# Bias rows of the attention: stored to DRAM once, then copied from DRAM to DRAM, one head at a time

## Chip, cores and metric

The kernel runs on one core of a Trainium2 chip. The metric is the time of one execution on the device in microseconds (us); lower is better. Engines are named as the profile names them: PE (TensorE, matmuls), DVE (VectorE), ACT (ScalarE), POOL (GpSimd) and SP (SyncE, which here only issues DMAs). POOL's DMAs go through the queue software_dynamic (q0), SP's through hardware_dynamic (q1); both are carried by the same 16 DMA engines.

## The reference

Two layers, each of three parts that add to x (512 tokens of width 1024, float32):

```python
for l in range(DEPTH):          # DEPTH = 2
    x = x + 0.5 * swiglu_ffn(rms_norm(x, ffn1_norm_w[l]), ffn1_w_gate[l], ffn1_w_up[l], ffn1_w_down[l])
    x = x + hybrid_mixer(rms_norm(x, mix_norm_w[l]), l, ...)
    x = x + 0.5 * swiglu_ffn(rms_norm(x, ffn2_norm_w[l]), ffn2_w_gate[l], ffn2_w_up[l], ffn2_w_down[l])
```

The mixer runs an mLSTM, a state-space branch with convolutions, and a differential attention of four heads, and projects their outputs back. What the change touches is the bias of the attention, which depends only on the distance of query and key:

```python
rel = q_pos[:, None] - k_pos[None, :]
bias = rel_bias[t5_bucket(rel)]            # per head
logits = (q @ k.T) * scale + bias          # -inf where rel < 0
```

## The kernel before

**Phases.** The list PHASES runs f1, mx, f2 for layer 0 and again for layer 1: `ffn`, `mixer`, `ffn`. Activations stay in SBUF with the 1024 features on 8 tiles of 128 partitions x 512 tokens.

**Matmuls.** Every large product is made of three matmuls (`mm3`, L127 to L129) of operands that are split into a high and a low part. Weights come in blocks of 1 MB: `load` (L108) lets SP fetch a block into `raw`, of which there are two buffers; `split` (L121, L122) casts half a block on ACT into `whi` and subtracts on DVE into `wlo`, of each of which there are three buffers. So SP can issue a block only when the block two before it has been split, and a split waits until PE is done with the one three before it. In the first FFN, PE needs about 11 us for a block: the loop over f runs 22 blocks for gate and up, and 11 more follow for the down product.

**The bias.** `build_bias(h)` is called inside the first FFN of layer 0, at f = 3, 5, 7 and 9, for h = 0 to 3. For h = 0 it multiplies a one-hot matrix `oh` with `rel_bias` in two small matmuls, which gives one row of 640 values per head, and copies them to `bias_row`, a tile of 4 partitions in SBUF. Each call then lets POOL copy one head's row 128 times into `bias_dram[h]` (128 x 640 values, 320 KB). The mixer reads it back with a step of 639 in `load_pair` (L510), so that each of 128 partitions of the tile `T` gets its row shifted by one; T is added to the logits in `soft` (L528), ACT makes the exponentials `pt` (L531) from them, PE transposes these (L545), ACT copies them to `aT` (L547) and PE multiplies with the values (L556).

**Order.** The order of the instructions on each engine is not written by hand. A scheduler places the whole program, both layers in one piece, by its own estimates of durations and of when tiles come free; `load`, `split` and the first loads ask it for a high priority. Each engine, and each DMA queue's issuing engine, then works its list from top to bottom and waits at semaphores. The mixer of layer 0 and that of layer 1 are the same code, but their orders differ in the kernel before. Apart from the weights SP and POOL issue in a mixer: the stores of q and k to `qk_dram` (L402) and their reload as `st` (L504), T (L510), the mask loads `sS` (L631) with the row added to them (L632), and the like for `D` (L748, L749).

Of the kernel before, what the change touches and what calls it, by code (L numbers as in the profile page):

```python
# [10 lines left out]
F32 = mybir.dt.float32  # L11
# [3 lines left out]
ALU = mybir.AluOpType  # L15
# [4 lines left out]
P = 128  # L20
# [8 lines left out]
NEG = -1.0e30  # L29
NREL = 640  # L30
# [14 lines left out]
def hybrid_kernel(ctx, tc, aps, phases):  # L45
    nc = tc.nc
    pe, act, dve, pool = nc.tensor, nc.scalar, nc.vector, nc.gpsimd

    const = ctx.enter_context(tc.tile_pool(name="const", bufs=1))
# [7 lines left out]
    dram = ctx.enter_context(tc.tile_pool(name="dram", bufs=1, space=DRAM))  # L57

    def acc():
        return acc_pool.tile([P, S], F32, name="acc", tag="acc")  # L60

    def aux():
        return aux_pool.tile([P, S], F32, name="aux", tag="aux")
# [40 lines left out]
    def load(src, soon=True):  # L104
        n = src.shape[1]
        with tc.high_priority() if soon else nullcontext():
            raw = wp.tile([P, 2 * WPC], F32, name="raw", tag="raw", bufs=2)
            nc.sync.dma_start(out=raw[:, :n], in_=src)  # L108
        return raw

    def split(raw, lo, n, eng=dve):
        return split_parts(raw, ((lo, n),), eng)

    def split_parts(raw, parts, eng=dve):
        with tc.high_priority():
            hi = wp.tile([P, WPC], F32R, name="whi", tag="whi", bufs=3)
            lw = wp.tile([P, WPC], F32R, name="wlo", tag="wlo", bufs=3)
            to = 0
            for lo, n in parts:
                t = slice(to, to + n)  # L120
                act.copy(hi[:, t], raw[:, lo:lo + n])  # L121
                eng.tensor_tensor(lw[:, t], raw[:, lo:lo + n], hi[:, t].bitcast(F32), ALU.subtract)  # L122
                to += n
        return hi, lw

    def mm3(out, lh, ll, rh, rl, first, last):
        pe.matmul(out, lh, rh, start=first, stop=False)  # L127
        pe.matmul(out, lh, rl, start=False, stop=False)  # L128
        pe.matmul(out, ll, rh, start=False, stop=last)  # L129


    def prep(d, wcol):
        w = pv[:, wcol + d:wcol + d + 1]
        act.activation(xh[d], x[d], AF.Copy, scale=w)
        dve.scalar_tensor_tensor(xl[d], x[d], w, xh[d].bitcast(F32), ALU.mult, ALU.subtract)  # L135
        if d == 0:
            act.activation(sqacc, x[d], AF.Square)
        else:
            sq = tp.tile([P, S], F32, name="sq", tag="t0", bufs=2)
            act.activation(sq, x[d], AF.Square)  # L140
            dve.tensor_tensor(sqacc, sqacc, sq, ALU.add)
# [16 lines left out]
    def rms_of_x():  # L158
        ps = aux()
        for j in range(NB):  # L160
            pe.matmul(ps[:, j:j + 1], sqacc[:, j * P:(j + 1) * P], ones[:, 0:1], start=True, stop=True)
        rst = tp.tile([P, NB], F32, name="rst", tag="rst", bufs=2)
        dve.tensor_copy(rst, ps[:, 0:NB])
        rstd(rst, DM)
        return rst

    def spread(rst):
        pb = aux()
        for j in range(NB):
            pe.matmul(pb[:, j * P:(j + 1) * P], rst[:, j:j + 1].broadcast_to([P, P]), ident, start=True, stop=True)  # L170
        act.copy(rsb, pb)


    def ffn(l, which, nxt, first):
        with tc.tile_pool(name=f"g{l}{which}", bufs=1) as gp:
            gh, gl = [], []
            for f in range(KF):
                if f == 0:

                    halves = [((512 * r, 512), (1024 + 512 * r, 512)) for r in range(2)]  # L180
                    raw = raw0 if first else load(aps["wgu"][l, which, f])
                    pp = [acc(), aux()]
                    for r in range(2):
                        hi, lw = split_parts(raw, halves[r])
                        for k in range(4):
                            if 4 * r + k == KD - 1:
                                rst = rms_of_x()
                            for u in range(2):
                                c = slice((u * 4 + k) * P, (u * 4 + k + 1) * P)
                                mm3(pp[u], hi[:, c], lw[:, c], xh[4 * r + k], xl[4 * r + k], 4 * r + k == 0, 4 * r + k == KD - 1)  # L190
                    spread(rst)
                else:
                    raw = load(aps["wgu"][l, which, f], f > 1 or not first)
                    pp = []
                    for u in range(2):
                        hi, lw = split(raw, u * 1024, 1024)
                        ps = aux() if u else acc()
                        for k in range(KD):
                            c = slice(k * P, (k + 1) * P)
                            mm3(ps, hi[:, c], lw[:, c], xh[k], xl[k], k == 0, k == KD - 1)  # L200
                        pp.append(ps)
                if first and 3 <= f <= 9 and f % 2:
                    build_bias(f // 2 - 1)
                gs = tp.tile([P, S], F32, name="gs", tag="t0", bufs=2)
                dve.tensor_tensor(gs, pp[0], rsb, ALU.mult)  # L205
                act.activation(gs, gs, AF.Silu)
                us = tp.tile([P, S], F32, name="us", tag="t1", bufs=2)
                dve.tensor_tensor(us, pp[1], rsb, ALU.mult)  # L208
                dve.tensor_tensor(us, us, gs, ALU.mult)
                h = gp.tile([P, S], F32R, name=f"gh{f}")  # L210
                lo = gp.tile([P, S], F32R, name=f"gl{f}")
                act.copy(h, us)
                dve.tensor_tensor(lo, us, h.bitcast(F32), ALU.subtract)
                gh.append(h)
                gl.append(lo)
            ps = None
            for c in range(KD * KF // 16):
                raw = load(aps["wdn"][l, which, c])
                for half in range(2):
                    hi, lw = split(raw, half * 1024, 1024)  # L220
                    for s in range(8):
                        d, k = divmod(c * 16 + half * 8 + s, KF)
                        if k == 0:
                            ps = aux() if d % 2 else acc()
                        cc = slice(s * P, (s + 1) * P)
                        mm3(ps, hi[:, cc], lw[:, cc], gh[k], gl[k], k == 0, k == KF - 1)
                        if k == KF - 1:
                            dve.scalar_tensor_tensor(x[d], ps, 0.5, x[d], ALU.mult, ALU.add)
                            if nxt is None:
                                nc.sync.dma_start(out=aps["out"][:, d, :], in_=x[d])  # L230
                            else:
                                prep(d, nxt)


    bias_dram = dram.tile([4, P, NREL], F32, name="bias_dram")
# [1 line left out]
    row_dram = dram.tile([DEPTH, 12, S], F32, name="row_dram")  # L237
    qk_dram = dram.tile([2, 2, 2, 4, 32, S], F32, name="qk_dram")

    bias_row = const.tile([4, NREL], F32, name="bias_row")  # L240

    def build_bias(h):

        if h == 0:
            with tc.tile_pool(name="bb", bufs=1) as bp:
                oh = bp.tile([33, NREL], F32, name="oh")
                nc.sync.dma_start(out=oh, in_=aps["oh"])
                rb = bp.tile([33, 4], F32, name="rb")
                dve.memset(rb, NEG)
                nc.sync.dma_start(out=rb[0:32], in_=aps["rel_bias"])  # L250
                dve.tensor_scalar(rb, rb, -1.0, None, ALU.mult)
                for a, b in ((0, 320), (320, 640)):
                    ps = aux()
                    pe.matmul(ps[0:4, :b - a], rb, oh[:, a:b], start=True, stop=True)
                    dve.tensor_copy(bias_row[:, a:b], ps[0:4, :b - a])
        pool.dma_start(out=bias_dram[h:h + 1], in_=bias_row[h:h + 1, None, :].broadcast_to([1, P, NREL]))

    def mixer(l, nxt):
        pvl, bcl = l * PV_N, l * BC_N
# [592 lines left out]
    for n, (kind, l) in enumerate(phases):  # L852
        nxt = None
        if n + 1 < len(phases):
            nxt = phases[n + 1][1] * PV_N + wcols[phases[n + 1][0]]
        if kind == "mx":
            if n == 0:
                for h in range(4):
                    build_bias(h)
            with ExitStack() as ctx2:  # L860
                mixer(l, nxt)
        else:
            ffn(l, 0 if kind == "f1" else 1, nxt, n == 0)
# [103 lines left out]
```

## Time and profile before

| | before |
|---|---|
| timed runs | 2048.39, 2056.11, 2056.96 us; median 2056.11 |
| profiled execution | 2051.0 us, span of its instructions 2048.9 us |
| PE busy | 1993.5 us, 97% of the span |
| DVE, ACT, POOL busy | 49%, 34%, 2% |
| granted clock of PE | 0.986 on average, 1.0 is 2.4 GHz |
| DMA | 209.13 MB, mean 102 GB/s |

The span runs from the first to the last instruction. A busy share is an average over stages, so it is read by stretches: where PE has no work, or works at a lower granted clock, the chain of waits says what it was waiting for. A DMA has a time to landing, from its issue until its data are there, and its packets have a share of the 16 DMA engines; a large share with few GB/s means that packets take long.

### The profile page before, as it was taken

To read this page: it belongs to the slowest core of one execution; us is meant where nothing else is said; L and a number is where in the kernel's file an instruction comes from. 1 tells how busy PE (TensorE), PEld (TensorE's weight loads), DVE (VectorE), ACT (ScalarE), POOL (GpSimd) and SP (SyncE) were. 2 spreads that over 40 slices of the span, in tenths; PEclk is the share of its full clock that TensorE was granted. 3 is DMA by queue.
4 is the path that set the end of the run, shared out by engine and by line. 5 is a ranking of instruction groups with operands and counts; after the bars stand their busy time and mean duration, and the time that the engine had idled before them with its cause. 6 is when DMAs were issued, how large, how long until landed. Compare 5 with 4: busy or idle time off the path is not lost.

```text
span 2048.9 us, 23668 instructions
## 1 busy us (share of the span) xinstructions
PE 1993.5 (97%) x9654; PEld 1663.1 (81%) x9654; DVE 995.9 (49%) x1701; ACT 699.2 (34%) x1144; POOL 48.9 (2%) x94
## 2 busy tenths in 40 slices
PE   8779999999799999999999999999999999999999
PEld 6668888898678888888888888888898888888887
DVE  5244433367566544443344444333687754444322
ACT  4123222243653433232223232223466433232211
POOL 0000000011100000000000000000110000000000
PEclk9989999999889999999999999999999999999999
DMA  5832222234631222222223222224464222222221
GB/s 176 58 112 103 93 92 103 84 128 135 160 83 40 96 102 103 92 93 103 99 87 103 87 99 103 97 89 129 146 160 124 63 83 103 88 98 103 103 103 62
DMA packets 48040, 209.13 MB, mean 102 GB/s; under 512 B 4843, under 2 KB 17419, under 8 KB 27068
## 3 DMA queue, kind: packets, MB, share of 16 engines
q1 hardware_dynamic: 41148, 187.38, 26.5%
q0 software_dynamic: 6784, 20.24, 6.1%
q8 instruction: 76, 1.25, 0.3%
q14 instruction: 32, 0.26, 0.0%
HBM read 193.66 MB, written 7.65 MB: 98 GB/s over the span
## 4 chain that ended last, share of the span: by engine, by line
PE 93%; DMA 4%; DVE 1%; ACT 1%; issue 0%; SPq 0%; ACTq 0%; POOLq 0%; DVEq 0%
PE acc L127 17%; PE acc L129 17%; PE acc L128 17%; PE aux L127 12%; PE aux L129 12%; PE aux L128 12%; DMA raw<-wgu 2%; PE aux L774 1%; PE po L556 1%; PE po L762 1%; PE aux L645 1%; PE aux L545 0%; DMA sS<-cn 0%; DMA D<-cn 0%; PE aux L524 0%
## 5 line engine op out<-in xcount | busy, mean ns | idle before, releaser
L121 ACT CAST whi<-raw 128x1024 fp32r<-128x1024 f32 (+2 forms) x344 | 350.7, 1022 | 1019.0 <-PE acc L128 419.3
L122 DVE TENSOR_TENSOR wlo<-raw,whi 128x1024 fp32r<-128x1024 f32 (+2 forms) x344 | 407.5, 1187 | 370.0 <-ACT whi L121 369.6
L127 PE MATMUL acc<-xh,whi 128*128 128x512 f32 x896 | 354.0, 395 | 30.4 <-ACT whi L121 22.1
L128 PE MATMUL acc<-xl,whi 128*128 128x512 f32 x896 | 353.3, 394 | 0.0
L129 PE MATMUL acc<-xh,wlo 128*128 128x512 f32 x896 | 352.5, 393 | 0.0
L127 PE MATMUL aux<-xh,whi 128*128 128x512 f32 x704 | 274.4, 390 | 0.0
L129 PE MATMUL aux<-xh,wlo 128*128 128x512 f32 x704 | 274.4, 390 | 0.0
L128 PE MATMUL aux<-xl,whi 128*128 128x512 f32 x704 | 274.3, 390 | 0.0
L127 PEld LDWEIGHTS acc<-xh,whi 128*128 128x128 f32 x896 | 169.8, 190 | 65.5 <-ACT whi L121 23.1
L129 PEld LDWEIGHTS acc<-xh,wlo 128*128 128x128 f32 x896 | 169.7, 189 | 34.9 <-DVE wlo L122 0.8
L128 PEld LDWEIGHTS acc<-xl,whi 128*128 128x128 f32 x896 | 170.2, 190 | 34.1 <-DVE xl L135 0.3
L208 DVE TENSOR_TENSOR us<-aux,rsb 128x512 f32<-128x512 f32 x88 | 60.8, 691 | 271.7 <-PE aux L129 271.7
L129 PEld LDWEIGHTS aux<-xh,wlo 128*128 128x128 f32 x704 | 132.5, 188 | 27.7
L127 PEld LDWEIGHTS aux<-xh,whi 128*128 128x128 f32 x704 | 132.5, 188 | 27.5
L128 PEld LDWEIGHTS aux<-xl,whi 128*128 128x128 f32 x704 | 132.3, 188 | 27.5
L205 DVE TENSOR_TENSOR gs<-acc,rsb 128x512 f32<-128x512 f32 x88 | 60.9, 692 | 180.9 <-PE acc L129 176.9
L127 PE MATMUL acc<-gh,whi 128*128 128x512 f32 x352 | 138.7, 394 | 0.0
L127 PE MATMUL aux<-gh,whi 128*128 128x512 f32 x352 | 138.7, 394 | 0.0
L129 PE MATMUL acc<-gh,wlo 128*128 128x512 f32 x352 | 138.0, 392 | 0.0
L129 PE MATMUL aux<-gh,wlo 128*128 128x512 f32 x352 | 138.0, 392 | 0.0
L128 PE MATMUL acc<-gl,whi 128*128 128x512 f32 x352 | 136.6, 388 | 0.0
L128 PE MATMUL aux<-gl,whi 128*128 128x512 f32 x352 | 136.6, 388 | 0.0
(266 smaller groups left out, 2564.3 us busy)
## 6 DMA issues: line engine op xcount, KB each, us to landing
raw<-wgu SPq DMA_DIRECT2D x87, 1024.0 KB, 4.8
raw<-wdn SPq DMA_DIRECT2D x44, 1024.0 KB, 4.8
raw<-win SPq DMA_DIRECT2D x12, 1024.0 KB, 5.0
raw<-winf SPq DMA_DIRECT2D x12, 1024.0 KB, 4.8
raw<-wout SPq DMA_DIRECT2D x8, 1024.0 KB, 5.0
st<-qk_dram POOLq DMA_DIRECT2D x24, 256.0 KB, 6.2
qk_dram<-hl POOLq DMA_DIRECT2D x16, 256.0 KB, 3.6
sS<-cn SPq DMA_DIRECT2D x8, 512.0 KB, 6.1
```

Of the source, the lines that this page charges most:

```text
L121: act.copy(hi[:, t], raw[:, lo:lo + n])
L122: eng.tensor_tensor(lw[:, t], raw[:, lo:lo + n], hi[:, t].bitcast(F32), ALU.subtract)
L127: pe.matmul(out, lh, rh, start=first, stop=False)
L128: pe.matmul(out, lh, rl, start=False, stop=False)
L129: pe.matmul(out, ll, rh, start=False, stop=last)
L205: dve.tensor_tensor(gs, pp[0], rsb, ALU.mult)
L208: dve.tensor_tensor(us, pp[1], rsb, ALU.mult)
L556: pe.matmul(po[:, h * 64:(h + 1) * 64], at["a", n][:, j * P:(j + 1) * P], dv[j][:, (2 * p + h) * 64:(2 * p + h + 1) * 64], start=j == 0, s ...
L645: pe.matmul(py[:, j * P + hh * 64:j * P + hh * 64 + 64], sS[:, hh * S + j * P:hh * S + (j + 1) * P], XC[:, j, h * 64:(h + 1) * 64], start= ...
L762: pe.matmul(sp[:, :n], mk[h // 2][hp, j * P:(j + 1) * P], mq[h // 2][hp, j * P:S], start=True, stop=True)
L774: pe.matmul(pnv[:, n, :], D[:, at_(j, n)], V[:, j, h, :], start=j == 0, stop=j == n)
```

## The change

`build_bias` loses its argument and is called once, at f = 2. It makes the four rows as before, in a tile `row` that lives only in the function's pool (`bias_row`, which lived to the end of the kernel, is gone), and lets POOL store them to a new DRAM tile `brow_dram` (4 x 640 values, 10 KB). A new function `spread_bias(h)`, called at f = 5, 7, 9 and 11, copies one head's row 128 times from `brow_dram` into `bias_dram[h]`, from DRAM to DRAM, on POOL's queue. What stands in `bias_dram` and who reads it is unchanged.

```diff
-                if first and 3 <= f <= 9 and f % 2:
-                    build_bias(f // 2 - 1)
+                if first and f == 2:
+                    build_bias()
+                if first and 5 <= f <= 11 and f % 2:
+                    spread_bias(f // 2 - 2)
...
-    bias_row = const.tile([4, NREL], F32, name="bias_row")
-
-    def build_bias(h):
-
-        if h == 0:
-            with tc.tile_pool(name="bb", bufs=1) as bp:
...
-        pool.dma_start(out=bias_dram[h:h + 1], in_=bias_row[h:h + 1, None, :].broadcast_to([1, P, NREL]))
+    brow_dram = dram.tile([4, NREL], F32, name="brow_dram")
+
+    def build_bias():
+        with tc.tile_pool(name="bb", bufs=1) as bp:
+            oh = bp.tile([33, NREL], F32, name="oh")
+            nc.sync.dma_start(out=oh, in_=aps["oh"])
+            rb = bp.tile([33, 4], F32, name="rb")
+            dve.memset(rb, NEG)
+            nc.sync.dma_start(out=rb[0:32], in_=aps["rel_bias"])
+            dve.tensor_scalar(rb, rb, -1.0, None, ALU.mult)
+            row = bp.tile([4, NREL], F32, name="row")
+            for a, b in ((0, 320), (320, 640)):
+                ps = aux()
+                pe.matmul(ps[0:4, :b - a], rb, oh[:, a:b], start=True, stop=True)
+                dve.tensor_copy(row[:, a:b], ps[0:4, :b - a])
+            pool.dma_start(out=brow_dram, in_=row)
+
+    def spread_bias(h):
+
+        pool.dma_start(out=bias_dram[h], in_=brow_dram[h:h + 1].broadcast_to([P, NREL]))
```

The scheduler also places other instructions differently, in the mixer of layer 0. Line numbers behind the edit grow by up to 5. On POOL, the stretch from the last of layer 0's stores of q and k to its first mask rows stands like this before (Gm, Ps and V are small tiles that POOL fills):

```order
L402 DMA qk_dram<-hl_2922 128x512
L448 DMA row_dram<-ar 8x512
L462 MEMSET Gm 128x64
L469 MEMSET Ps 128x4
L504 DMA st<-qk_dram 32x4x512 x2
L485 DMA row_dram<-mr 4x128 x4
L504 DMA st<-qk_dram 32x4x512 x4
L510 DMA T<-bias_dram 128x512 x4
L802 MEMSET V 128x4 x4
L632 DMA sS<-row_dram 128x1024 x2
```

After the change POOL's list from the first bias copy on is this, down to the first of the eight stores of q and k:

```order
L257 DMA brow_dram<-row 4x640
L261 DMA bias_dram<-brow_dram 128x640 x4
L467 MEMSET Gm 128x64
L474 MEMSET Ps 128x4
L515 DMA T<-bias_dram 128x512 x4
L807 MEMSET V 128x4 x4
L407 DMA qk_dram<-hl_2890 128x512
```

The four spreads stand together right behind the store, and the four loads of T and the fills have moved from behind the reload of q and k to ahead of its store.

SP's list at the start of layer 0's mixer (win, winf and wout are the mixer's weights, cn holds the mask that sS is filled with) is before:

```order
L108 DMA raw<-win 128x1088 x2
L108 DMA raw<-win 128x2048 x2
L108 DMA raw<-winf 128x2048 x4
L108 DMA raw<-win 128x2048 x2
L108 DMA raw<-winf 128x2048
L745 DMA row<-row_dram 128x512
L108 DMA raw<-winf 128x2048
L745 DMA row<-row_dram 128x512
L108 DMA raw<-win 128x2048
L631 DMA sS<-cn 128x8x128 x2
```

After the change the same place reads:

```order
L108 DMA raw<-win 128x1088 x2
L108 DMA raw<-win 128x2048
L636 DMA sS<-cn 128x8x128 x2
L108 DMA raw<-win 128x2048
L108 DMA raw<-winf 128x2048 x4
L108 DMA raw<-win 128x2048
L750 DMA row<-row_dram 128x512 x2
L108 DMA raw<-win 128x2048
L108 DMA raw<-winf 128x2048 x2
L636 DMA sS<-cn 128x8x128
```

The first two mask loads have moved ahead of the fourth win load, and the third one ahead of the last two. In layer 1, SP's and POOL's lists read like the ones after the change already in the kernel before.

## Rows read from the trace of the kernel before

**Rows 1.** Page: busy us of each engine; PE's granted clock in 40 slices.
```profile
PE 1993.5 (97%) x9654; PEld 1663.1 (81%) x9654; DVE 995.9 (49%) x1701; ACT 699.2 (34%) x1144; POOL 48.9 (2%) x94
...
PEclk9989999999889999999999999999999999999999
```

**Rows 2.** Stretches in FFN 1: length, busy of PE, PEld, DVE, ACT, POOL; clock, DMA share, GB/s.
```profile
60.00:80.00 20.00, 20.00 (x90) 16.56 (x89) 7.82 (x10) 5.38 (x7) 1.88 (x4) 1.00 0.99 34
...
90.70:112.80 22.10, 0.00 (x0) 0.00 (x0) 0.01 (x1) 1.09 (x2) 0.00 (x0) 0.62 0.91 95
```

**Rows 3.** Tile bias_row: ns min/median/max of one, first and last start; time to landing.
```profile
L256 POOL DMA_DIRECT2D bias_dram<-bias_row x4: 529/546/697, 59.6 to 61.4; - x4
...
DMA to landing us min/median/max: 14.4/32.4/49.0
```

**Rows 4.** DMA queues from 50 to 120: packets, MB, share of 16 engines.
```profile
q0 software_dynamic: 320, 1.31, 63.7%
```

**Rows 5.** The chain that ended last, 56 to 130: start us, us, what.
```profile
65.67 45.94 DMA raw<-wgu
111.71 1.05 ACT whi L121
```

**Rows 6.** Timeline of PE around the gap: start us, us, what [idle before, releaser].
```profile
90.28 0.39 PE L129 MATMUL aux<-xh,wlo 128*128 128x512 f32 x1
112.81 0.80 PE L127 MATMUL acc<-xh,whi 128*128 128x512 f32 x1 [22.14 <-ACT whi L121]
...
116.86 0.39 PE L127 MATMUL acc<-xh,whi 128*128 128x512 f32 x1
```

**Rows 7.** Timeline of PE: first matmul of layer 0's mixer and of its FFN 2.
```profile
398.90 0.29 PE L127 MATMUL acc<-whi,xh 128*128 128x272 f32 x1
...
694.71 0.39 PE L127 MATMUL acc<-xh,whi 128*128 128x512 f32 x1
```

**Rows 8.** Stretches: both mixers, and the slowest piece of layer 0's.
```profile
398.90:694.71 295.81, 276.35 (x1627) 236.82 (x1626) 189.51 (x468) 138.15 (x315) 23.19 (x43) 0.94 0.38 110
1419.54:1682.59 263.05, 261.29 (x1626) 226.96 (x1625) 187.39 (x468) 137.96 (x315) 23.21 (x43) 1.00 0.42 124
...
544.00:580.00 36.00, 24.43 (x86) 19.61 (x87) 19.84 (x71) 15.32 (x50) 1.83 (x2) 0.53 0.36 89
```

**Rows 9.** PE's waits in layer 0's mixer: us in total, times, longest.
```profile
PE aux L524 <- issue: 6.4, 1, 6.4
PE po L556 <- ACT aT L547: 4.9, 5, 2.3
```

**Rows 10.** Timelines of ACT and POOL: first softmax exponential and T, layers 0 and 1.
```profile
515.38 0.40 ACT L531 ACTIVATE pt<-L,mx 128x128 f32<-128x128 f32 x1
...
1504.60 0.40 ACT L531 ACTIVATE pt<-L,mx 128x128 f32<-128x128 f32 x1 [2.30 <-DVE mx L528]
...
500.57 2.21 POOL L510 DMA_DIRECT2D T<-bias_dram  x4
...
1420.31 2.20 POOL L510 DMA_DIRECT2D T<-bias_dram  x4 [0.30 <-issue]
```

**Rows 11.** DMA issues, whole span: broadcasts of a DRAM row, median to landing.
```profile
row<-row_dram SPq DMA_DIRECT2D x8, 256.0 KB, 6.1
```

**Rows 12.** Line 510, T from DRAM: one issue in ns; time to landing.
```profile
L510 POOL DMA_DIRECT2D T<-bias_dram x8: 546/556/577, 500.6 to 1422.0; - x8
...
DMA to landing us min/median/max: 4.8/8.6/12.3
```

**Rows 13.** DMA queues from 547 to 556, with one broadcast of DRAM rows (sS).
```profile
q0 software_dynamic: 227, 0.77, 41.8%
```

**Rows 14.** PE's longest wait in layer 1's mixer.
```profile
PE aux L662 <- ACT bt L659: 0.9, 1, 0.9
```

**Rows 15.** SP's waits in layer 1's mixer: the one ahead of sS.
```profile
SPq L631 <- PE aux L129: 3.7, 1, 3.7
```

More of the change, by code (lines that the diff above doesn't have):

```diff
@@ L238, in hybrid_kernel @@
     qk_dram = dram.tile([2, 2, 2, 4, 32, S], F32, name="qk_dram")
-    bias_row = const.tile([4, NREL], F32, name="bias_row")
-    def build_bias(h):
-        if h == 0:
-            with tc.tile_pool(name="bb", bufs=1) as bp:
[L246 to L255, printed above, removed]
-        pool.dma_start(out=bias_dram[h:h + 1], in_=bias_row[h:h + 1, None, :].broadcast_to([1, P, NREL]))
+    brow_dram = dram.tile([4, NREL], F32, name="brow_dram")
[15 more added lines that the diff above has]
+        pool.dma_start(out=bias_dram[h], in_=brow_dram[h:h + 1].broadcast_to([P, NREL]))
     def mixer(l, nxt):
@@ L857, in hybrid_kernel @@
             if n == 0:
+                build_bias()
                 for h in range(4):
-                    build_bias(h)
+                    spread_bias(h)
             with ExitStack() as ctx2:
```

## Prediction

> **What bounds the kernel now.** First the page: TensorE (PE) is busy for 97% of the span [rows 1], so a change pays only where PE stands still or runs below full clock. The page's row of the granted clock shows two such places, slice 3 and slices 11 and 12 of 40 (about 51 us each) [rows 1]. The rest is a matmul stream that this edit doesn't touch.
>
> The first place is inside the first FFN. The table by stretches shows PE at 0.00 us busy from 90.70 to 112.80, while the DMA engines are busy for 0.91 of the time and move only 95 GB/s; from 60 to 80 they are busy for 0.99 and move 34 GB/s [rows 2]. Busy engines that move almost nothing are held by slow packets. The tile's rows say whose: four copies of bias_row into bias_dram are issued at 59.6 to 61.4 and land after 14.4 to 49.0 us [rows 3]. The queue row gives the price: 320 packets of POOL's queue take 63.7% of 16 engines in 70 us, 713 us of engine time, 2.23 us each [rows 4]. Each of these copies reads one partition of SBUF 128 times. The weight load that starts at 65.67 meanwhile takes 45.94 us, and its cast at 111.71 waits for it [rows 5], and PE, whose last matmul starts at 90.28, for the cast until 112.81 [rows 6].
>
> The second place is the layer 0 mixer. Its first projection matmul starts at 398.90 and the next FFN's first at 694.71 [rows 7]: 295.81 us. The layer 1 mixer does the same work in 1419.54 to 1682.59: 263.05 us. The table by stretches splits the difference of 32.76: PE is busy 276.35 against 261.29 us (clock 0.94 against 1.00), so 15.06 us is slower matmuls, and idle 19.46 against 1.76, so 17.70 us is waiting [rows 8]. Most of it lies in 544 to 580, where PE is busy 24.43 of 36 us at a clock of 0.53 [rows 8]. PE's largest waits in this mixer are those of the attention, 6.4 us ahead of its logits and 4.9 us for the transposed probabilities [rows 9]. The attention starts late here: the first softmax exponential is at 515.38, 116.5 us into the mixer, against 1504.60, 85.1 us into the other, and the bias tiles T are issued at 500.57, behind the stores of q and k, but at 1420.31 in layer 1, at the very start [rows 10]. So in layer 0 the softmax chain meets few projections that could fill PE's gaps.
>
> **The change, step by step.** *Removed: four copies out of one partition.* PE's last matmul starts at 90.28 and takes 0.39; cast and hand-over take 1.10 (111.71 to 112.81) [rows 5, 6]. So a cast at 89.6 would have left no gap, and a load that starts at 65.67 has 23.9 us to land; it took 45.94, and 22.14 us of idle time followed. After the gap PE starts at half its clock, 1.2 of 2.4 GHz: the nine matmuls from 112.81 to 116.86 take 4.05 us [rows 6], where PE at full clock does 90 in the 20 us from 60 to 80 [rows 2], 0.22 to 0.23 each: 2.0 us lost. Together 24.1 us on the path.
>
> *Added: one 10 KB store and four copies from DRAM to DRAM.* The calls of the spreads stand at f = 5, 7, 9 and 11, but nothing on POOL stands between them: in the built program all four follow the store at once. The bias matmuls move one weight block (some 11 us) earlier; counted back from 59.6 [rows 3] the store goes out near 48, and the spreads a few us later, once it has landed. No row shows a copy from DRAM to DRAM. The nearest are broadcasts of one DRAM row over 128 partitions, 256 KB in a median of 6.1 us [rows 11], and the T loads from DRAM, 4.8 to 12.3 us with four in flight [rows 12]. Lower bound for all four spreads: in 547 to 556 a 512 KB broadcast from DRAM took 41.8% of 16 engines over 9 us for 227 packets, 0.27 us each [rows 13], an eighth of 2.23; 320 of those are 85 us of engine time, 5.3 us on 16 engines. Upper bound: four in series at 6.1 x 320/256 = 7.6 us, 30.5 us. I take 15 us, 12.3 x 320/256, since the T loads too are four in flight. The weight load that meets them has the same two raw buffers and three split tiles ahead of it, so about 24 us to land: 15 costs nothing, while after 30.5, with 5 of its own, it would be up to 11 us late. These buffers are the cover; without them the 15 us would be paid. A gain beyond the stall is not possible here, as PE has no other gap in this FFN. The bias matmuls, their copies and the 10 KB store are the same or off the path: nothing.
>
> The Trainium skill, DMA: Bandwidth & Descriptors, section Anatomy of one DMA, gives a fit of 2.0 us plus bytes over 436 GB/s, whatever the source. By it four copies of 320 KB take about 5 us (an estimate) from SBUF as from DRAM, and there would be nothing to gain in the FFN; the 49.0 us of [rows 3] contradict that, so the measurement decides. Its section Where 436 GB/s comes from gives 27.2 GB/s for one of 16 SBUF ports; by that 1.31 MB out of one port take 48 us (an estimate), which is what the trace shows.
>
> *Moved: the whole layer 0 mixer.* The diff has no line there, yet the scheduler orders it anew. POOL now issues T ahead of the eight stores of q and k, SP issues the first two mask loads sS behind the third win load instead of after ten more weight loads and two row loads, and the softmax moves up among the convolutions. Read entry by entry, the new order of this mixer on PE (1640 entries from its first), DVE (475), ACT (318), SP (35) and POOL (43) is the one that layer 1 has in the kernel before. So its price needn't be guessed: the same instructions in the same order took 263.05 us [rows 8], and the step is worth 32.76. Its waits are in layer 1's rows too: PE's longest there is 0.9 us [rows 14], and SP waits 3.7 us for the last FFN matmul ahead of the first sS, with a weight load queued behind [rows 15], without a gap on PE. What layer 0 adds is that sS waits for the 10 KB store and T for the spreads, both over 300 us old by then: nothing. Bounds: nothing, if the loss belongs to layer 0 and not to its order, and 32.76. I take the whole.
>
> Sum: 24.1 + 32.8 = 56.9 us. The profiled execution took 2051.0 us (span 2048.9), so it becomes 1994.1. The timed runs lie at 2048.39, 2056.11 and 2056.96, the median 5.1 above the profiled one. No row shows where these 5 us sit: in the two lost stretches they would go too (1994), elsewhere they stay (1999). I predict the middle, 1996.5.
>
> **Rivals.** *The copies stay slow.* 128 reads of one DRAM row on 16 engines could serialise like those of one partition. Against it: 0.27 against 2.23 us for a packet, both of them broadcasts [rows 4, 13]. For it: here the writes go to DRAM as well, which no row shows together with such a read. With packets of 2 us the stall stays whole and only the mixer gains: 1996.5 + 24.1 = 2021; halfway, 2008. The skill's same page (Latency and other measured facts) reports copies in DRAM that fall from 207 to 103 GB/s at some row pitches, which it puts down, unverified, to streams that meet in one channel. By 103 GB/s the four would take 13 us (an estimate), inside the 24; no run here shows it.
>
> *The mixer keeps its loss*, by some cause of layer 0 that isn't order: only the FFN gains, 1996.5 + 32.8 = 2029. For it: one execution of each order is all there is. Against: the waits of [rows 9] are the attention's, which is what the order moves.
>
> *Nothing moves:* the copies stall as before and the mixer loses as before, about 2053.
>
> *Slower:* the DRAM copies hold the queues longer than the SBUF ones did. One place, the weight load in the FFN, whose packets take turns with theirs. To lose net, the stall must eat the mixer's 32.8 us as well: the four copies would need some 82 us instead of 49, 3.7 us a packet instead of 2.23, and 14 times the 0.27 of the DRAM broadcast. At 4.5 us a packet they take 99 us, 50 more than now: 2021 + 50 = 2071.
>
> **How the numbers follow.** Forecast (both places gone) 0.80, within 1989 to 2003 by the spread of the runs before; copies slow in part or whole 0.07; mixer loss kept in part or whole 0.06; nothing 0.04; slower 0.03. The range is 1988 to 2010: above the forecast it takes in the 11 us of the copies' upper bound and leaves out the worse rivals. About 0.5%, 10 us, is what a measurement of this kernel can tell from no change. The first three cases are faster by more: 0.93, with 0.04 for the same and 0.03 for slower.
>
> **What would show it.** In the profile of after: the four spreads land within about 15 us (over 25 is wrong); between 40 and 130 ACT waits for a weight load no longer than some us, and PE stays at clock 1.00; the mixer of layer 0 takes 263 us from its first matmul to the next FFN's, without its stretch at half clock, and begins some 24 us earlier than before; layer 1 is unchanged. The prediction is wrong if the spreads take tens of us, or if layer 0's mixer, in layer 1's order, still needs over 270 us.

## The result, and the profile after

| | before | after |
|---|---|---|
| timed runs, us | 2048.39 to 2056.96, median of 4 2053.71 | 1993.20 to 1994.57, median of 4 1993.81 |
| profiled execution, us (span) | 2051.0 (2048.9) | 1993.66 (1991.9) |
| first projection matmul of layer 0's mixer | 398.90 | 374.20 |
| first matmul of the FFN behind it | 694.71 | 637.72 |

The ratio is 0.9713 with a 95% interval of 0.9695 to 0.9731: 59.9 us less by the medians, 57.0 by the two spans. The forecast was 1996.5 us in 1988 to 2010.

The page of after, in the lines of [rows 1] (busy us of each engine; PE's granted clock in 40 slices):

```profile
PE 1976.7 (99%) x9654; PEld 1652.2 (83%) x9654; DVE 993.8 (50%) x1701; ACT 699.0 (35%) x1144; POOL 49.6 (2%) x95
...
PEclk9999999999999999999999999999999999999999
```

The two dips, in slice 3 and slices 11 and 12, are gone, and PE is busy for 16.8 us less with the same 9654 matmuls, since none of them runs at half clock any more.

The line of the four copies from DRAM to DRAM (engine, what, count, ns of one issue, first and last start; then us to landing), as [rows 3] for before:

```profile
L261 POOL DMA_DIRECT2D bias_dram<-brow_dram x4: 526/532/575, 50.6 to 52.2; - x4
...
DMA to landing us min/median/max: 3.7/5.0/5.8
```

All four have landed by 58 us, some 7 us from the first issue, where before it took 50.8 (59.6 to 61.4 plus 49.0 [rows 3]). POOL's queue from 40 to 110 (packets, MB, share of 16 engines), as [rows 4]:

```profile
q0 software_dynamic: 352, 1.32, 6.0%
```

That is 67 us of engine time for 352 packets, 0.19 us each instead of 2.23. And the stretches of [rows 2, 8] in the kernel after (length, busy of PE, PEld, DVE, ACT, POOL; clock, DMA share, GB/s):

```profile
90.00:112.80 22.80, 22.80 (x103) 18.86 (x102) 10.77 (x13) 7.41 (x9) 0.00 (x0) 1.00 0.31 111
374.20:637.72 263.52, 261.46 (x1627) 226.85 (x1625) 187.37 (x468) 137.89 (x315) 23.34 (x43) 1.00 0.42 124
637.72:1362.56 724.84, 724.84 (x3202) 598.14 (x3200) 309.46 (x380) 210.77 (x257) 0.00 (x0) 1.00 0.27 95
```

Where PE stood still for 22.1 us it is now busy throughout at full clock. Layer 0's mixer takes 263.52 us, as layer 1's did in [rows 8] (263.05). The stretch from there to layer 1's mixer takes 724.84 us, and took 724.83 before (694.71 to 1419.54): nothing moved outside the two places. The mixer begins 24.70 us earlier and is 32.29 us shorter, together 56.99 of the 57.0 that the span lost. POOL issues the bias tiles T at the start of the mixer, and the first softmax exponential follows 85.1 us in (116.5 before, [rows 10]). POOL's and ACT's timelines:

```profile
374.67 2.15 POOL L515 DMA_DIRECT2D T<-bias_dram  x4
...
459.26 0.40 ACT L536 ACTIVATE pt<-L,mx 128x128 f32<-128x128 f32 x1 [2.30 <-DVE mx L533]
```

So the theory is that there are two separate causes: the one-partition source stalls a weight load, and the scheduler's order of the mixer, which hangs on how the copies are written, costs the rest. The experiments take each of them away alone.

### The profile page after: what moved, and what is told of

The parts are those of the page before. It is cut to its first block, busy times and chain, and to the rows that moved or that the text cites. A ratio compares the mean times of both kernels' runs of the same rounds, so it can differ in the third digit from the quotient of the medians.

```text
span 1991.9 us, 23652 instructions
## 1 busy us (share of the span) xinstructions
PE 1976.7 (99%) x9654; PEld 1652.2 (83%) x9654; DVE 993.8 (50%) x1701; ACT 699.0 (35%) x1144; POOL 49.6 (2%) x95
## 4 chain that ended last, share of the span: by engine, by line
PE 97%; DMA 1%; DVE 1%; ACT 1%; issue 0%; SPq 0%; POOLq 0%
PE acc L127 18%; PE acc L129 17%; PE acc L128 17%; PE aux L127 13%; PE aux L129 13%; PE aux L128 13%; PE po L561 1%; PE aux L779 1%; DMA D<-cn 1%; PE po L767 1%; PE aux L529 0%; PE aux L650 0%; DMA D<-row_dram 0%; PE aux L550 0%; PE side L767 0%; PE aux L702 0%
```

## The experiments

### Stall and order, each alone: four kernels

Which order the scheduler gives layer 0's mixer depends on how the copies are written, and that made all four combinations buildable. In all four each copy reads one SBUF partition. Two set them apart in time through a small VectorE operation that depends on data of its own block; two let them queue together. In the two with a tile for each head PE's list of the mixer stands in layer 1's order, and in the two where all copies read one tile, in the order of before.

**Early, together, one tile** is after with the copies' source put back (the store to DRAM goes too; `...` marks what is left out):

```
...
-        pool.dma_start(out=bias_dram[h], in_=brow_dram[h:h + 1].broadcast_to([P, NREL]))
+        pool.dma_start(out=bias_dram[h:h + 1], in_=row_sb[h:h + 1, None, :].broadcast_to([1, P, NREL]))
```

> After's calls (rows made at f = 2, copies called at f = 5 to 11), but each copy reads one SBUF partition 128 times, as before; no store to DRAM. In the built order the layer 0 mixer is back in the order of before. Theory (the one-partition source makes the stall, and the stall's copies make the order): the four copies are issued near 49 and need some 49 us, a weight load that starts near 54 lands over 40 us later, PE stands still for about 22 us around 80 to 102, the mixer takes about 296 us, total about 2050. Rival (moving the calls to other places is what helped): no stall, about 2026 if the mixer's 32 us stay, 1994 if both are gone.

Measured: 2050.72 us median of 10 runs, ratio to before 0.9999 (0.9989 to 1.0008). PE's timeline shows the stall, moved one block forward with the calls (start us, us, what, idle before and its releaser):

```profile
101.39 0.79 PE L127 MATMUL acc<-xh,whi 128*128 128x512 f32 x1 [22.24 <-ACT whi L121]
```

The mixer takes 294.74 us. Moving the calls is worth nothing; it is what the copies read, here one tile in SBUF, that changes both.

**Spaced, a tile for each head:**

```
...
-        pool.dma_start(out=bias_dram[h:h + 1], in_=bias_row[h:h + 1, None, :].broadcast_to([1, P, NREL]))
+        z = gp.tile([4, 1], F32, name=f"z{h}")
+        dve.tensor_scalar(z, us[0:4, 0:1], 0.0, None, ALU.mult)
+        one = gp.tile([4, NREL], F32, name=f"one{h}")
+        dve.tensor_scalar(one, bias_row, z, None, ALU.add)
+        pool.dma_start(out=bias_dram[h:h + 1], in_=one[h:h + 1, None, :].broadcast_to([1, P, NREL]))
```

> Copies out of one SBUF partition as before, but 22 us apart: each head's row goes through a small tile of its own, whose VectorE operation waits for data of its own block f (3, 5, 7, 9). The layer 0 mixer stands in layer 1's order in the build. Theory (a one-partition copy does harm only when several are queued together; one takes 12 to 14 us, two blocks of the FFN take 22, and a weight load has 24 us to land): every copy lands 12 to 15 us after its issue, no gap of PE in the first FFN over 1 us, mixer 263 us, total about 1994. Rival (the slow packets by themselves hold up weight loads, however few copies): a gap of 3 to 6 us at each copy, 2005 to 2018. Second rival (the mixer's loss follows the copies' source and not its order): mixer 296, about 2027.

Measured: 1999.20 us median of 4 runs, ratio 0.9748 (0.9732 to 0.9764). The copies' line, and the stretches of the first FFN and the mixer:

```profile
DMA to landing us min/median/max: 13.5/13.7/13.9
```

```profile
40.00:375.93 335.93, 335.93 (x1468) 274.56 (x1466) 141.43 (x171) 94.33 (x115) 2.30 (x4) 1.00 0.40 98
375.93:643.18 267.25, 263.09 (x1626) 228.32 (x1625) 187.17 (x468) 137.78 (x315) 23.18 (x43) 0.99 0.42 122
```

Each copy is as slow as before (13.5 to 13.9 us), PE has no gap, and the mixer is near its short time: slow packets, one copy at a time, cost PE nothing, and a DRAM source isn't needed. The miss is 5 us of total: by the spans this kernel is 5.9 us behind after, 1.7 up to the mixer, 3.7 in it and 0.4 behind it. In the mixer PE waits once for a VectorE operation, a wait that after doesn't have (waits of PE: us, times, longest):

```profile
PE acc L127 <- DVE cwh L579: 2.3, 1, 2.3
```

The other two kernels with added VectorE operations show it too (2.3 and 2.9 us). VectorE's list isn't quite layer 1's in them: this operation runs 16 to 17 us into the mixer (here at 392.1), and 2.0 us into it in after (376.2). The comparison below is among these kernels.

**Spaced, one tile** writes in place instead, so that copy h + 1 also waits for copy h; the copies read `bias_row` again:

```
...
-        one = gp.tile([4, NREL], F32, name=f"one{h}")
-        dve.tensor_scalar(one, bias_row, z, None, ALU.add)
+        dve.tensor_scalar(bias_row, bias_row, z, None, ALU.add)
```

> The copies of the spaced kernel (one SBUF partition each, far apart), but all four read the one tile bias_row, into which a small VectorE operation writes before each copy. The scheduler then keeps the order of before in the layer 0 mixer: on PE all 1640 entries stand as in before. So the stall is taken away and the order is kept. Theory (the mixer's 32 us belong to its order): no gap of PE in the first FFN, mixer 292 to 296 us, total 2024 to 2029. Rival (the mixer was slow because of what the stall or the late copies left behind): mixer about 263, total about 1996.

Measured: 2032.33 us median of 4 runs, ratio 0.9911 (0.9894 to 0.9928), 3.3 us above the forecast's 2029. The stretches of the first FFN, the mixer and its slow piece:

```profile
40.00:377.41 337.41, 337.41 (x1473) 276.05 (x1472) 141.31 (x170) 94.86 (x115) 1.78 (x3) 1.00 0.36 97
377.41:675.92 298.51, 276.88 (x1626) 237.77 (x1625) 190.18 (x469) 137.90 (x315) 23.73 (x44) 0.93 0.40 110
520.00:560.00 40.00, 27.24 (x109) 21.68 (x108) 21.62 (x77) 18.39 (x56) 3.70 (x6) 0.58 0.43 105
```

There is no gap in the FFN, yet the mixer takes 298.51 us and has its stretch near half clock (0.58, where 544 to 580 had 0.53 in [rows 8]). PE's two longest waits in it are those of [rows 9], and the third is that of the spaced kernel:

```profile
PE aux L527 <- issue: 6.7, 1, 6.7
PE po L559 <- ACT aT L550: 3.9, 5, 1.5
PE acc L127 <- DVE cwh L578: 2.9, 1, 2.9
```

**Together, a tile for each head** fills z by a memset instead of from the block's data:

```
...
-        dve.tensor_scalar(z, us[0:4, 0:1], 0.0, None, ALU.mult)
+        dve.memset(z, 0.0)
```

> The counterpart: four copies out of one SBUF partition each, queued together as before, but each from a tile of its own, with which the scheduler puts the layer 0 mixer into layer 1's order (all 1640 entries of PE). So the stall is kept and the order is taken away. Theory: a gap of PE of about 22 us in the first FFN, 2 us of half clock behind it, mixer 263 us, total 2016 to 2020. Rival (stall and mixer are one loss): 2050 or 1994.

Measured: 2024.80 us median of 4 runs, ratio 0.9871 (0.9856 to 0.9886), 4.8 us above the forecast's 2020; like the two kernels before it, it carries some us that the forecasts, worked out from before and after, leave out. PE's timeline at the gap, and the mixer:

```profile
113.19 0.80 PE L127 MATMUL acc<-xh,whi 128*128 128x512 f32 x1 [22.92 <-ACT whi L121]
```

```profile
401.43:667.38 265.95, 261.65 (x1627) 227.00 (x1625) 187.18 (x468) 137.74 (x315) 23.17 (x43) 1.00 0.42 123
```

The stall is whole and the mixer is short. The four side by side, by the profiled executions:

| | span us | PE idle in the FFN | mixer 0 | first exponential, into the mixer |
|---|---|---|---|---|
| stall, old order (before) | 2048.9 | 22.14 | 295.81 | 116.5 |
| stall, new order | 2022.1 | 22.92 | 265.95 | 87.5 |
| no stall, old order | 2030.6 | 0 | 298.51 | 122.2 |
| no stall, new order (spaced) | 1997.8 | 0 | 267.25 | 88.9 |

Among the last three, which carry added operations of the same kind, the stall is worth 24.3 us (2022.1 less 1997.8; 25.5 up to the mixer, less 1.3 in it) and the order 32.8 (2030.6 less 1997.8); the forecast had 24.1 and 32.76. They are two losses, and neither brings the other about on the chip. They hang together only in the scheduler.

The no-stall, old-order kernel also hints at what the scheduler reckons. POOL's timeline:

```profile
61.63 0.70 POOL L259 DMA_DIRECT2D bias_dram<-bias_row  x1 [61.19 <-DVE bias_row L258]
192.80 0.56 POOL L259 DMA_DIRECT2D bias_dram<-bias_row  x1 [130.48 <-DVE bias_row L258]
324.59 0.52 POOL L259 DMA_DIRECT2D bias_dram<-bias_row  x1 [131.23 <-DVE bias_row L258]
```

The copies land after 13.6 to 14.1 us, but the in-place operation that follows each of them stands some 130 us further on in VectorE's list, as if the scheduler reckoned that long for a copy. That it puts T and the softmax off for this reason is not shown: the kernels with a tile for each head have the same copies and get the new order.

### T early, the softmax where it was

```
-                pool.dma_start(out=T[:, r * S:(r + 1) * S], in_=src)
+                with tc.high_priority():
+                    pool.dma_start(out=T[:, r * S:(r + 1) * S], in_=src)
```

> The kernel before, with one thing changed: the T loads of the mixers are issued at high priority, so that POOL issues them right behind the bias copies, over 300 us before their use; PE's list for the layer 0 mixer stays that of before but for 94 of 1640 entries. The copies in the FFN stay slow, so the stall of 22 us stays. Theory (the place of the softmax among the projections in the lists makes the mixer's loss, not the arrival of T): mixer 290 to 296 us, total 2045 to 2056. Rival (T arrives too late at 500.57, and that is what holds the attention): mixer about 263, total about 2020.

Measured: 2036.68 us median of 4 runs, ratio 0.9931 (0.9913 to 0.9949), between the two forecasts (2045 to 2056, and about 2020), for the most part for another reason than T. POOL issues three of the four T loads from 387.76 on and the last at 442.18, but has only three of the bias copies in the FFN; the fourth goes out inside the mixer:

```profile
387.76 1.09 POOL L511 DMA_DIRECT2D T<-bias_dram  x2 [326.72 <-PE aux L129]
388.85 0.54 POOL L256 DMA_DIRECT2D bias_dram<-bias_row  x1
```

That makes it a trial with three copies in a row, with a gap of 10.09 us in place of 22.14. The mixer takes 291.42 us; below it stand a piece of it and PE's longest wait there:

```profile
387.30:678.72 291.42, 276.66 (x1627) 236.71 (x1626) 188.95 (x468) 138.15 (x315) 23.77 (x44) 0.94 0.42 113
540.00:560.00 20.00, 14.68 (x53) 11.19 (x53) 14.56 (x52) 12.19 (x41) 0.00 (x0) 0.50 0.06 25
...
PE aux L546 <- DVE pt L538: 4.2, 4, 1.6
```

T is issued up to 113 us earlier than in [rows 10], and the mixer is 4.4 of the 32 us shorter. The wait of 6.4 us ahead of the logits, the longest in [rows 9], is gone, yet the piece at half clock is still there (0.50), and the first exponential still comes 117.5 us into the mixer. So neither that wait nor T's arrival makes the loss; of the causes named, the softmax's place in the lists is left.

### Two copies from SBUF

This is the kernel after, with heads 0 and 1 (`if h < 2`) copied from DRAM and heads 2 and 3 from one SBUF partition each.

> After, with heads 2 and 3 copied out of one SBUF partition each and heads 0 and 1 from DRAM. The mixer stays in layer 1's order. Three such copies in a row (the kernel with T first) landed after 37.4 us, held a weight load for 33.9 us and cost 10.1 us of idle PE; four 49.0, 45.9 and 22.1; one at a time 13.9, 13.9 and 0. Theory (the stall is the load's delay beyond the 24 us of cover): two land after 24 to 30 us, the load takes 21 to 26, idle PE 0 to 2 us, total 1993 to 1997. Rival (each slow copy costs its share, 5 us): idle PE about 10 us, total about 2004.

Measured: 1993.53 us (one run). The copies' landing, the weight loads' (x17, 40 to 200), and ACT's timeline at the load that was late:

```profile
DMA to landing us min/median/max: 13.9/18.8/23.6
```

```profile
DMA to landing us min/median/max: 4.7/4.8/21.1
```

```profile
75.73 1.05 ACT L121 CAST whi<-raw 128x1024 fp32r<-128x1024 f32 x1 [11.03 <-DMA raw<-wgu]
```

The cast waits 11 us for the load, and PE doesn't notice. Together with the other runs this gives the size of the cover:

| copies from one partition, in a row | last landed after | longest load | PE idle | load less idle |
|---|---|---|---|---|
| 1 (spaced) | 13.9 | 13.9 | 0 | |
| 2 | 23.6 | 21.1 | 0 | |
| 3 (T early) | 37.4 | 33.9 | 10.09 | 23.8 |
| 4 (before) | 49.0 | 45.94 | 22.14 | 23.8 |
| 4 (a tile for each head) | 48.1 | 46.7 | 22.92 | 23.8 |

PE idles for what a load takes beyond 23.8 us, the same in all three; the prediction's slack was 23.9. The rival, a price for each copy, falls with the first two lines.

### Slow because of one partition, or because of SBUF?

```
...
+                for h in range(4):
+                    ps = aux()
+                    pe.matmul(ps[:, :b - a], rb[:, h:h + 1].broadcast_to([33, P]), oh[:, a:b], start=True, stop=True)
+                    dve.tensor_copy(wide[:, h, a:b], ps[:, :b - a])
...
+        pool.dma_start(out=bias_dram[h], in_=wide[:, h])
```

> The bias rows are made on all 128 partitions (eight matmuls of 128 x 320 instead of two of 4 x 320, eight copies out of PSUM on VectorE), and the four copies go from 128 SBUF partitions to DRAM, with no broadcast. The layer 0 mixer stands in layer 1's order. Theory (it is the single partition that is slow, not SBUF as a source): four copies of 320 KB land in about 5 to 15 us, packets of POOL's queue well under 1 us instead of 2.23, no gap of PE, total about 1994 plus some 3 us for six more matmuls in full float32, 1997. Rival (only a source in DRAM is fast): stall of about 22 us, mixer 263, about 2018.

Measured: 1998.04 us median of 4 runs, ratio 0.9742 (0.9723 to 0.9761). POOL's queue from 40 to 120, and the copies:

```profile
q0 software_dynamic: 320, 1.31, 4.3%
...
bias_dram<-wide POOLq DMA_DIRECT2D x4, 320.0 KB, 3.1
```

The same 320 packets and 1.31 MB take 55 us of engine time, 0.17 us each against 2.23, and land after 3.1 us: spread over 128 partitions SBUF is as good a source as DRAM. Two things differ here at once: 128 partitions are read instead of one, and every byte once instead of 128 times. Repeated reads of one DRAM row are fast (0.19 us); repeated reads of one partition against plain reads of it were not separated. The mixer takes 263.10 us and starts 5.1 us later than after's; the bias matmuls take 5.1 us instead of 1.2, and the rest came with a clock of 0.98 between 20 and 120, so six more matmuls cost 5 and not 3 us. The change's own way, two matmuls and a 10 KB store, is the cheaper.

### A busy queue without slow packets

```
...
+        for c in range(7):
+            pool.dma_start(out=scr_dram[7 * h + c], in_=brow_dram[h:h + 1].broadcast_to([P, NREL]))
```

> After, with every copy from DRAM to DRAM made eight times (seven of them into a scratch buffer that nobody reads): 32 copies of 320 KB in a row on POOL's queue. Theory (what stalls a weight load is the length of the packets, 2.23 us, not that the queue is busy): by the four copies that landed in about 7 us the 32 keep the queue busy for some 50 us, packets stay near 0.2 to 0.3 us, weight loads land in 10 to 12 us instead of 4.8, no gap of PE, total 1993 to 1997. Rival (it is the time that the queue is busy, over 24 us): a weight load lands over 40 us late, gap of about 22 us, total about 2018.

Measured: 1994.33 us (one run). POOL's queue from 50 to 128, the weight loads' landing, and the stretch:

```profile
q0 software_dynamic: 2560, 10.49, 65.1%
```

```profile
DMA to landing us min/median/max: 4.7/4.9/16.9
```

```profile
40.00:130.00 90.00, 90.00 (x397) 73.52 (x396) 42.48 (x51) 26.48 (x34) 17.45 (x33) 1.00 0.83 210
```

The 32 copies take 812 us of engine time in 78 us, more than the 713 of the four slow ones [rows 4], and for longer (78 us, not 50 as expected; 0.32 us a packet). The loads land after at most 16.9 us (10 to 12 were expected) and PE doesn't stop. So the queue's share doesn't tell a stall. The time of one packet alone doesn't either: in the spaced kernel POOL's queue from 50 to 150 shows

```profile
q0 software_dynamic: 320, 1.31, 44.1%
```

which is 706 us of engine time and 2.2 us a packet, as in [rows 4], and PE has no gap. What tells it is how long a load issued behind the slow packets takes to land, against the 23.8 us of cover.

## Why the prediction was right, step by step

- **The stall:** right in cause and size. 24.70 us forward against 24.1, and 24.3 between the two kernels that differ in it alone. The slack of a load, worked out as 23.9, measured 23.8.
- **The copies from DRAM:** mis-sized, at no cost. I took 15 us for all four by the T loads; they took 7, near the lower bound of 5.3 that came from the price of a packet (0.27 us; measured 0.19). The packet of a like transfer was the better row than the landing time of a smaller one. Even eight times as many did not stall PE.
- **The order of the mixer:** 32.29 us against 32.76. That equal lists take equal time is now shown, by the no-stall, old-order kernel, which kept the 32 us, and by the stall, new-order one, which lost them. That what costs is the softmax's place and not T's arrival was argued from the waits; the early T supports it, with three of the four T loads early. The wait of 6.4 us, which the prediction named first, isn't what the loss hangs on, since it went with the early T and the loss stayed. Which of the old order's waits starts the half-clock stretch was not separated.
- **The rivals:** copies that stay slow, a mixer that keeps its loss, and a loss net all needed something that the profile of after shows not to be so. The rival slower by 3.7 us a packet had packets take turns with the load's; the trace bears that out (see the last section), and it fell because the packets from DRAM are short.
- **The median:** I added half of the 5.1 us by which the three runs shown exceed the profiled one. That offset was a matter of three runs: in the 24 runs of the kernel before that there are by now, the median is 2050.4, at the profiled 2051.0. The sum without it, 1994.1, is within 0.3 us of the median of after. The step that failed is taking an offset of a small sample for something that the kernel has.

## What to carry to other kernels

A DMA that reads one SBUF partition many times should be spread over partitions, bounced through DRAM, or kept apart in time. What it costs is read from the time that a load issued behind it takes to land, held against that load's slack; neither the queue's share nor the time of a packet tells it alone. Where a scheduler sets the order, compare the built lists before and after an edit even in stages that the diff doesn't touch: here more than half of the gain sat in one, and the same instructions in the order of another layer gave its price beforehand.

## What the runs showed of the hardware

**A load behind slow copies lands when they do.** The weight load issued behind the copies landed 0.2 to 1.3 us after the last of them, whether there were two, three or four: before's at 111.6, with the last copy issued at 61.4 and landed 49.0 later, at 110.4; with three, at 99.2 (65.35 plus 33.89) against about 98; with two, its cast starts at 75.73, and the last copy, issued at 51.84, landed 23.6 later. In the chain that ended last with T early:

```profile
65.35 33.89 DMA raw<-wgu
```

The data themselves come late, and not only the report that they are there. In the kernel before, the load was issued at 65.67. The DMA queues from 65.6 to 75.4, and then from 75.4 to 110.4, when the last copy landed (packets, MB, share of 16 engines):

```profile
q0 software_dynamic: 65, 0.25, 90.4%
...
q0 software_dynamic: 223, 0.90, 86.3%
q1 hardware_dynamic: 199, 1.53, 10.3%
```

For 9.7 us no packet of SP's queue (q1) moves at all. After that 199 of its packets, of this load and the next one, stand beside 223 of POOL's, nearly one to one, though theirs take 0.29 us each (10.3% of 16 engines in 35 us) and POOL's some 2.2. The Trainium skill, DMA: Bandwidth & Descriptors, section Queues, rings and completion order, says that engines take turns between queues by packets, and also that a completion increment lands only after every earlier write of its engine, across queues. From 75.4 on the trace agrees with the first; the second isn't needed for a delay of this size, and no run here separates what it adds. What holds the load back for the first 9.7 us stays open. Behind the 32 copies from DRAM, with 0.32 us a packet, a load took at most 16.9 us.

**The rate of one partition.** Four copies of 320 KB took 50.8 us from the first issue to the last landing [rows 3], 25.8 GB/s, and one alone 13.7 us; the same bytes from 128 partitions landed in 2.7 to 3.3 us each. The four read four partitions, one each, and landed one after another, so the figure is that of one partition at a time; whether neighbouring partitions read together would be faster no run shows.

**The spread of the times goes with the order.** Kernels with the mixer's old order vary by 3.5 to 9.1 us between runs (no stall 3.5 in 4 runs, T early 4.1 in 4, early copies 4.5 in 10, before 9.1 in 24), those with the new one by 0.8 to 1.7 in 4 runs each, the one with the stall among them (1.4). The prediction asked in which of the two places the spread sits; by these few runs it is the mixer and not the stall. What in the mixer varies stays open.
